# A two-layer RWKV-7/S5 trunk: solve columns moved to PSUM, lower weight parts reloaded, GpSimd's one-tensor operations given to ScalarE

## The chip, the cores and the metric

The kernel runs on one core of one Trainium2 chip. The metric is the device time of one execution in microseconds (us). TensorE is PE in the profile, VectorE is DVE, ScalarE is ACT, GpSimd is POOL and SyncE, which only issues DMAs here, is SP. Each of these engines works through its own instructions strictly in the order in which they were written; an instruction that has to wait for another engine holds up everything behind it on its own engine.

## The reference, cut to what matters

The input is 1024 tokens of 1024 channels in float32. Layer 0 is an RWKV-7 time mixer, layer 1 an S5 state-space mixer; each is followed by a squared-ReLU MLP of width 4096, and each sub-layer by a layer norm. The change lies in layer 0's mixer alone:

```python
xx = jnp.pad(x, ((0, 0), (1, 0), (0, 0)))[:, :-1] - x
xr = x + xx * mu[0]                      # likewise xw, xk, xv, xa, xg
r = xr @ wr
w_pre = (w0 + jnp.tanh(xw @ w1) @ w2).astype(f32)
decay = jnp.exp(-jnp.exp(-jax.nn.softplus(-w_pre) - 0.5))
k = xk @ wk
v = xv @ wv
a = jax.nn.sigmoid(a0 + (xa @ a1) @ a2)
g = jax.nn.sigmoid(xg @ g1) @ g2
k = k * (1.0 + (a - 1.0) * k_a)
def step(state, inp):
    r_t, w_t, k_t, v_t, a_t, b_t = inp
    sa = jnp.einsum('bhvk,bhk->bhv', state, a_t)
    state = (state * w_t[:, :, None, :] + sa[..., None] * b_t[:, :, None, :]
             + v_t[..., None] * k_t[:, :, None, :])
    return state, jnp.einsum('bhvk,bhk->bhv', state, r_t)
_, o = lax.scan(step, s0, seq_in)
```

The recurrence is not run token by token. It is cut into chunks of 64 tokens, and what the tokens of a chunk do to each other is a triangular system that is solved for each chunk and head.

## The kernel before, in words

**Products in two parts.** Every large matrix product takes its operands as an upper part (float32 rounded to the PE's fast format) and a lower part (what the rounding left). `wload` fetches a block of 128x512 weights into `wraw`, ScalarE copies it to the upper part `whi` (L146), VectorE subtracts to get the lower part `wlo` (L147), and `mm3` issues three matmuls (L175): upper by upper, upper by lower, lower by upper. Two buffers hold `wraw`, three `whi` and three `wlo`. All weights are fetched in this way each time they are used, 720 blocks in all.

**Two halves.** The tokens are treated as two halves of 512. `rwkv_proj(0)` and `rwkv_proj(1)` make the projections of each half with the same weights: `rates` (the decay and `a`, two weight blocks a half), `gate` (two), `square` (`wk` and `wr`, 16 blocks each) and the products with `wv` (16): 52 blocks a half that the change concerns. `mixes` makes the shifted inputs, x times (1 - mu) on ScalarE (L266) plus the shifted x times mu, either in one operation on VectorE (L268) or in two on GpSimd (L271, L272). `half_sigmoid` (L325) turns a tanh into a sigmoid on GpSimd. Results go to DRAM (`scr`) and come back for the recurrence.

**Eight units.** The recurrence runs in eight units, each of 256 tokens and 8 of the 16 heads. For each unit `elem` loads r, k, sg and a from `scr` (L485) and scales them, among others with `a` times k_a plus `kam` on GpSimd (L527); `amat` makes the triangular matrices; `invert` solves them; `chain` carries the state over the chunks (PE pR L672, pX L677, pU L682, with ScalarE and VectorE copies between them, L668 to L679); `gnorm` normalises the result, mostly on GpSimd (L733 to L739).

**The solve.** `invert` handles diagonal blocks of 32 by 32. The solved columns `xh` lie in half of the SBUF tile `x1`. Thirty steps of two VectorE operations follow: a product of a matrix column `xa` and solved rows into `tmp` (L608) and its addition to the rows below (L610), of 15 to 128 elements a partition. After that come two transposes (L614, L615), small matmuls into a PSUM tile `pv1` of pool `pl` (one buffer, tag "l"), and copies. The layer norms use the same buffer for `pm`, `pq` and `pr`.

**What sets the order.** A scheduler orders each engine's instructions by priorities (`rank`) and a model of their times; dependencies between rotating buffers follow the order in which the program names them. The projections of the second half, the output product `wo(0)` and the MLP have low priority, so they fill PE between the steps of the units. The units end at about 1060 us of the span; the MLPs, the S5 mixer and its products follow.

Of the kernel before, what the change touches and what calls it, by code (L numbers as in the profile page):

```python
# [8 lines left out]
F32 = mybir.dt.float32  # L9
# [9 lines left out]
HT = 512  # L19
# [51 lines left out]
def trunk(ctx, tc, A):  # L71
# [32 lines left out]
    V.tensor_scalar(kam, pv[:, PV.index("k_a")], -1.0, 1.0, op0=ALU.mult, op1=ALU.add)  # L104

    mum = cp.tile([128, 6, KT], F32, name="mum")
    V.tensor_scalar(mum, pv[:, 0:6], -1.0, 1.0, op0=ALU.mult, op1=ALU.add)

    def vec(n, k):
        i = PV.index(n)  # L110
        return pv[:, i, k : k + 1]
# [45 lines left out]

    def wload(src, kt, n):
        step = 512 // n
        out = []  # L160
        for k0 in range(0, kt, step):
            raw = wp.tile([128, step, n], F32, tag="wraw", name="wraw", bufs=2)
            SP.dma_start(raw, src[:, k0 : k0 + step])
            hi = wp.tile([128, step, n], F32R, tag="whi", name="whi")
            lo = wp.tile([128, step, n], F32R, tag="wlo", name="wlo")
            nw[0] += 1
            split(raw, hi, lo, G if nw[0] % WLG[0] in WLG[1] and WLG[2] <= nw[0] < WLG[3] else V)
            out += [(hi[:, k], lo[:, k]) for k in range(step)]
        return out
# [59 lines left out]
    def rwkv_proj(H):  # L229
# [33 lines left out]
        def mixes(j, dst=None):  # L263
            for k in range(KT):
                m = tp.tile([128, HT], F32, tag="m", name="m")
                S.mul(m, xs[k][:, 1:], mum[:, j, k : k + 1])  # L266
                if k % 4 in VM[H]:
                    V.scalar_tensor_tensor(m, xs[k][:, 0:HT], vec(f"mu{j}", k), m, op0=ALU.mult, op1=ALU.add)  # L268
                else:
                    m2 = tp.tile([128, HT], F32, tag="ev", name="m2", bufs=3)  # L270
                    G.tensor_scalar(m2, xs[k][:, 0:HT], vec(f"mu{j}", k), None, op0=ALU.mult)  # L271
                    G.tensor_add(m, m, m2)  # L272
                if dst:
                    split(m, *dst[k])
                    yield dst[k]
                else:
                    yield operand(m)
# [46 lines left out]
        def half_sigmoid(t):  # L324
            G.tensor_scalar(t, t, 0.5, 0.5, op0=ALU.mult, op1=ALU.add)  # L325

# [42 lines left out]
        def rates(n):  # L369

            if n % 4 == 0:
                w2[0] = wload(A["wa2"][:, n // 4], 4, 128)
            pp = [psd(), psd()]
# [10 lines left out]
        def gate(n):  # L384
            if n % 4 == 0:
                wg[0] = wload(A["g2a"][:, n // 4], 4, 128)
                rawb = wp.tile([128, 512], F32, tag="wraw", name="w2raw", bufs=2)
# [12 lines left out]
        def square(wn, out, xm, n):  # L400
            p = psd()
            dense(p, wload(A[wn][n], KT, 128), xm)
            e = tp.tile([128, HT], F32, tag="ev", name="ev", bufs=3)
            S.copy(e, p)  # L404
            store_out(out, n, e)
# [34 lines left out]
        for cb in range(4):  # L440
            pp = [psd(), psd()]
            for k0 in range(0, KT, 2):
                w = wload(A["wv"][cb][:, k0 : k0 + 2], 2, 256)
                for kk in range(2):
# [29 lines left out]
    def elem(m):  # L474
# [5 lines left out]
        for j in range(2):  # L480
# [45 lines left out]
            for i in range(2):  # L526
                G.tensor_scalar(kf[:, per(i)], a[:, per(i)], vec("k_a", n0 + i), kam[:, n0 + i : n0 + i + 1],  # L527
                                op0=ALU.mult, op1=ALU.add)
            G.tensor_mul(kf, kf, k)
# [55 lines left out]
    def invert(D):  # L585
# [5 lines left out]
        tmp = x1[:, 0].rearrange("p u j -> p (u j)")  # L591
        blk, xh = x1[:, 1], x1[:, 1].rearrange("p u j -> p (u j)")
        xv = xh.rearrange("p (t j) -> p t j", t=32)
# [771 lines left out]
```

## Time and profile before

| what | value |
|---|---|
| median of 3 runs | 2771.85 us (2769.56 to 2778.86) |
| the profiled execution's own time | 2764.91 us |
| its span, first to last instruction | 2763.2 us |
| its mean granted PE clock | 0.958 |
| PE matmul busy | 2604.9 us, 94% of the span |
| VectorE busy | 1884.5 us, 68% |
| ScalarE busy | 1109.5 us, 40% |
| GpSimd busy | 719.6 us, 26% |

A busy share is an average over stages, and PE counts as busy while a matmul is in its pipeline, at whatever clock. So the table says that PE is the engine to look at, and not yet where it loses time. The views used below are busy times by stretches of the span (us, then each engine's busy us and instruction count, then the granted PE clock, the DMA share and GB/s), groups of instructions (`x` count, busy us, mean ns, then the engine's idle time before them), one line's durations as min/median/max in ns, and the waits (us in total, times, longest).

### The profile page before, as it was taken

Reading aid. Unit: us, or ns where it says so; the run is one execution under the profiler, and the core shown is the slowest. Engines: PE = TensorE matmul, PEld = TensorE weight load, DVE = VectorE, ACT = ScalarE, POOL = GpSimd, SP = SyncE. Lnnn points to the kernel's source line nnn. Section 1 sums busy time; section 2 is a strip of 40 time slices with the busy share of each in tenths; the row PEclk is TensorE's granted clock in tenths of the full one; section 3 lists DMA queues with packets and bytes.
Section 4 is the critical chain, followed back from the end, with each engine's and each line's share of the span. In section 5 each row is a group of like instructions: output and inputs, shape, how many; then the busy total and the mean of one; then the engine's idle time right before and its main releaser. Section 6 shows DMA issues by size and latency. Waiting matters only on the chain.

```text
span 2763.2 us, 43707 instructions
## 1 busy us (share of the span) xinstructions
PE 2604.9 (94%) x16582; PEld 2096.5 (76%) x16582; DVE 1884.5 (68%) x3242; ACT 1109.5 (40%) x1952; POOL 719.6 (26%) x601
## 2 busy tenths in 40 slices
PE   7889989889899999989999999999999999999997
PEld 5779767678677877767776788778778887788886
DVE  7487788587787777998658554574765546755556
ACT  5445454544443333334432332344323323533333
POOL 5331664450352303233122001121220101210101
PEclk9989969889889999999999999999999999999998
DMA  3543443344222323555332633223343322333333
GB/s 115 184 147 112 139 162 102 109 138 135 77 81 81 100 85 124 154 145 159 96 122 99 203 96 98 89 88 102 117 160 112 99 96 84 119 96 97 98 95 100
DMA packets 200083, 318.63 MB, mean 115 GB/s; under 512 B 19520, under 2 KB 73920, under 8 KB 199872
## 3 DMA queue, kind: packets, MB, share of 16 engines
q1 hardware_dynamic: 199872, 315.83, 36.6%
q8 instruction: 131, 2.15, 0.3%
q14 instruction: 80, 0.66, 0.1%
HBM read 265.42 MB, written 50.33 MB: 114 GB/s over the span
## 4 chain that ended last, share of the span: by engine, by line
PE 45%; DVE 5%; issue 2%; POOL 1%; DMA 1%; ACT 0%; ACTq 0%; DVEq 0%; POOLq 0%
PE d L175 40%; PE py L1219 1%; PE py L1224 1%; DVE wlo L147 1%; PE pu L152 1%; DVE t L1187 1%; PE pbu L1175 1%; DVE hA L960 0%; DVE hB L960 0%; DVE t L1185 0%; POOL rl L944 0%; PE pq L849 0%; DMA wraw<-in_mw_dram 0%; PE pu L1164 0%; DVE qbuf L147 0%
## 5 line engine op out<-in xcount | busy, mean ns | idle before, releaser
L147 DVE TENSOR_TENSOR wlo<-wraw,whi 128x512 fp32r<-128x512 f32 x720 | 535.6, 745 | 443.7 <-ACT whi L146 424.8
L146 ACT CAST whi<-wraw 128x512 fp32r<-128x512 f32 x720 | 445.7, 620 | 975.4 <-PE d L175 637.2
L175 PE MATMUL d<-qbuf,whi 128*128 128x512 f32 (+1 forms) x2112 | 655.6, 393 | 20.9 <-DVE hA L960 9.4
L175 PEld LDWEIGHTS d<-qbuf,whi 128*128 128x128 f32 x2112 | 390.3, 190 | 117.7 <-DVE hA L960 17.0
L944 POOL TENSOR_TENSOR rl<-rl 128x512 f32<-128x512 f32 x128 | 158.6, 1239 | 1058.4 <-ACT rl L943 1018.1
L175 PE MATMUL d<-qbuf,wlo 128*128 128x512 f32 (+1 forms) x1056 | 409.3, 390 | 8.2 <-DVE wlo L147 8.0
L175 PE MATMUL d<-oAh,whi 128*128 128x512 f32 (+1 forms) x960 | 387.8, 408 | 9.6 <-ACT ev L404 7.2
L175 PE MATMUL d<-oAh,wlo 128*128 128x512 f32 (+1 forms) x960 | 387.2, 406 | 5.3 <-DVE wlo L147 5.1
L175 PE MATMUL d<-oAl,whi 128*128 128x512 f32 (+1 forms) x960 | 385.5, 404 | 1.4 <-DVE oAl L147 1.4
L175 PE MATMUL d<-oBh,wlo 128*128 128x512 f32 x704 | 278.3, 396 | 1.4 <-DVE wlo L147 1.4
L175 PE MATMUL d<-oBh,whi 128*128 128x512 f32 x704 | 278.8, 396 | 0.0
L175 PE MATMUL d<-oBl,whi 128*128 128x512 f32 x704 | 276.1, 392 | 0.0
L175 PEld LDWEIGHTS d<-qbuf,wlo 128*128 128x128 f32 x1056 | 200.6, 190 | 52.8 <-DVE wlo L147 11.7
L175 PEld LDWEIGHTS d<-oAh,whi 128*128 128x128 f32 (+1 forms) x960 | 185.1, 194 | 54.2 <-ACT ev L404 9.2
L175 PEld LDWEIGHTS d<-oAh,wlo 128*128 128x128 f32 (+1 forms) x960 | 184.9, 193 | 49.1 <-DVE wlo L147 8.6
L175 PEld LDWEIGHTS d<-oAl,whi 128*128 128x128 f32 (+1 forms) x960 | 184.8, 193 | 40.6 <-DVE oAl L147 2.1
L960 DVE TENSOR_TENSOR hB<-hB,d 128x512 f32<-128x512 f32 (+1 forms) x256 | 165.2, 650 | 68.9 <-PE d L175 65.8
L960 DVE TENSOR_TENSOR hA<-hA,d 128x512 f32<-128x512 f32 x240 | 162.5, 683 | 54.5 <-PE d L175 52.5
L175 PEld LDWEIGHTS d<-oBh,wlo 128*128 128x128 f32 x704 | 132.5, 188 | 33.8 <-DVE wlo L147 2.0
L175 PEld LDWEIGHTS d<-oBl,whi 128*128 128x128 f32 x704 | 132.7, 188 | 29.4 <-issue 0.5
L175 PEld LDWEIGHTS d<-oBh,whi 128*128 128x128 f32 x704 | 132.7, 189 | 29.1 <-issue 1.5
L147 DVE TENSOR_TENSOR qbuf<-rl,qbuf 128x512 fp32r<-128x512 f32 x128 | 99.0, 774 | 70.3 <-ACT qbuf L146 69.8
(371 smaller groups left out, 3877.1 us busy)
## 6 DMA issues: line engine op xcount, KB each, us to landing
wraw<-in_mw_dram SPq DMA_DIRECT2D x520, 256.0 KB, 2.7
wraw<-in_glu_dram SPq DMA_DIRECT2D x64, 256.0 KB, 2.6
wraw<-in_wk_dram SPq DMA_DIRECT2D x32, 256.0 KB, 3.1
wraw<-in_wr_dram SPq DMA_DIRECT2D x32, 256.0 KB, 3.1
wraw<-in_wv_dram SPq DMA_DIRECT2D x32, 256.0 KB, 3.4
yl<-s_y SPq DMA_DIRECT2D x32, 256.0 KB, 3.1
wraw<-in_wo_dram SPq DMA_DIRECT2D x32, 256.0 KB, 2.8
tb<-tB SPq DMA_DIRECT2D x16, 512.0 KB, 4.9
```

The source lines that it names most:

```text
L146: S.copy(hi, src)
L147: (e or V).tensor_sub(lo, src, hi.bitcast(F32))
L152: PE.matmul(out, x, idt, start=True, stop=True)
L175: bulk.append((PE.matmul(p, w, x, **kw).ins, x.shape[-1]))
L944: G.tensor_mul(r, r, r)
L960: V.tensor_add(z, z, p)
L1175: PE.matmul(p[qs, g2, ri], tb[:, g2, ri, qs], u[:, 2 * g2 + par], start=True, stop=True)
L1187: e.tensor_mul(t2[:, :, ri], x[:, :, 1 - ri], bw[:, l, g0:g1, ri : ri + 1].broadcast_to([128, g1 - g0, n]))
L1219: PE.matmul(p[64 * j : 64 * j + 64, g2], ug[f][:, 2 * g2 + par], tv[:, par, g2], start=g2 == 0, stop=False, skip_group_check=True)
L1224: PE.matmul(p[64 * j : 64 * j + 64, g2], hb[qs, 4 * f + g2, ri, 0:NSC], tcm[qs, g2, ri], start=False, stop=ri == 1, skip_group_check=True)
```

## The change

Four edits, all in layer 0's mixer:

1. `invert` takes `xh` from the PSUM pool `pl` (tag "l", the one buffer it shares with `pv1` and the layer norms' tiles). Before, `xh` was half of `x1`.
2. `wload` gets a key. The first time a block with a key is loaded (first half), its lower part is stored to a DRAM tile `low`. The second time (second half) the lower part is loaded from there into `wlo`, and VectorE's subtraction is left out; ScalarE still makes the upper part.
3. Of `mixes`, the multiplication by mu moves from GpSimd to ScalarE (18 instructions); the addition stays on GpSimd.
4. `half_sigmoid` (36 instructions) and the scaling of `a` in `elem` (32) move from GpSimd to ScalarE, the first with a constant tile `half` as its bias.

```diff
+    half = cp.tile([128, 1], F32, name="half")
+    V.memset(half, 0.5)
...
-    def wload(src, kt, n):
+    low = {}
+
+    def wload(src, kt, n, key=None):
...
+            kept = low.get((key, k0)) if key else None
             raw = wp.tile([128, step, n], F32, tag="wraw", name="wraw", bufs=2)
             SP.dma_start(raw, src[:, k0 : k0 + step])
...
-            split(raw, hi, lo, G if nw[0] % WLG[0] in WLG[1] and WLG[2] <= nw[0] < WLG[3] else V)
+            if kept is not None:
+                SP.dma_start(lo.bitcast(F32).rearrange("p k n -> p (k n)"), kept)
+                S.copy(hi, raw)
+            else:
+                split(raw, hi, lo, G if nw[0] % WLG[0] in WLG[1] and WLG[2] <= nw[0] < WLG[3] else V)
+                if key:
+                    low[key, k0] = dr.tile([128, 512], F32, name=f"low{len(low)}")
+                    SP.dma_start(low[key, k0], lo.bitcast(F32).rearrange("p k n -> p (k n)"))
...
-                    G.tensor_scalar(m2, xs[k][:, 0:HT], vec(f"mu{j}", k), None, op0=ALU.mult)
+                    S.mul(m2, xs[k][:, 0:HT], vec(f"mu{j}", k))
...
-            G.tensor_scalar(t, t, 0.5, 0.5, op0=ALU.mult, op1=ALU.add)
+            S.activation(t, t, AF.Identity, bias=half, scale=0.5)
...
-            dense(p, wload(A[wn][n], KT, 128), xm)
+            dense(p, wload(A[wn][n], KT, 128, f"{wn}{n}"), xm)
...
-                G.tensor_scalar(kf[:, per(i)], a[:, per(i)], vec("k_a", n0 + i), kam[:, n0 + i : n0 + i + 1],
-                                op0=ALU.mult, op1=ALU.add)
+                S.activation(kf[:, per(i)], a[:, per(i)], AF.Identity, bias=kam[:, n0 + i : n0 + i + 1],
+                             scale=vec("k_a", n0 + i))
...
-        blk, xh = x1[:, 1], x1[:, 1].rearrange("p u j -> p (u j)")
+        blk = x1[:, 1]
+
+        xh = pl.tile([128, HT], F32, tag="l", name="xh")
```

The loads for `rates`, `gate` and `wv` get keys in the same way as that of `square`.

The scheduler orders anew. On VectorE, in the solve of the fourth unit (`x_` is the tile `x1`, `wlo` a weight block's lower part), the program had before:

```order
L608 TENSOR_TENSOR x_4040<-xa,x_4040 128x110
L610 TENSOR_TENSOR x_4040<-x_4040 128x22x5
L147 TENSOR_TENSOR wlo<-wraw,whi 128x512
L608 TENSOR_TENSOR x_4040<-xa,x_4040 128x105
L610 TENSOR_TENSOR x_4040<-x_4040 128x21x5
L685 TENSOR_TENSOR st<-pU,st 128x256
L147 TENSOR_TENSOR wlo<-wraw,whi 128x512
L608 TENSOR_TENSOR x_4040<-xa,x_4040 128x120
L686 TENSOR_TENSOR st<-st,PL 128x256
L610 TENSOR_TENSOR x_4040<-x_4040 128x20x6
```

At the same steps of the same solve it now has:

```order
L623 TENSOR_TENSOR x_4149<-xa,xh 128x110
L625 TENSOR_TENSOR xh<-xh,x_4149 128x22x5
L623 TENSOR_TENSOR x_4149<-xa,xh 128x105
L625 TENSOR_TENSOR xh<-xh,x_4149 128x21x5
L623 TENSOR_TENSOR x_4149<-xa,xh 128x120
L700 TENSOR_TENSOR st<-pU,st 128x256
L625 TENSOR_TENSOR xh<-xh,x_4149 128x20x6
L701 TENSOR_TENSOR st<-st,PL 128x256
```

The subtractions for the second half's weights no longer stand between the steps, and each step has one SBUF input and one PSUM input where it had two from SBUF. From the first to the last step of this solve 30 other instructions stood between before, 8 do now.

On SP, in the second half's products with `wk` (`s_k` is k's place in DRAM, `vsa`, `ldk`, `lg`, `gt` loads for the units), the program had before:

```order
L163 DMA wraw<-in_wk_dram 128x512 x3
L365 DMA s_k<-ev 128x512
L163 DMA wraw<-in_wk_dram 128x512
L365 DMA s_k<-ev 128x512
L163 DMA wraw<-in_wk_dram 128x512
L365 DMA s_k<-ev 128x512
L485 DMA ldk<-s_k 128x2x256
L163 DMA wraw<-in_wk_dram 128x512
L749 DMA s_y<-gt 128x4x128
```

It now has:

```order
L498 DMA ldk<-s_k 128x2x256
L174 DMA wlo<-low_750 128x512
L169 DMA wraw<-in_wk_dram 128x512
L174 DMA wlo<-low_1319 128x512
L169 DMA wraw<-in_wk_dram 128x512
L669 DMA vsa<-s_v 64x2x256 x2
L378 DMA s_k<-ev 128x512
L174 DMA wlo<-low_1327 128x512
L169 DMA wraw<-in_wk_dram 128x512
```

Each weight block brings two loads instead of one, and the loads and stores of the units stand in the same queue behind them. Over the whole program SP issues 104 DMAs more, ScalarE has 86 instructions more, GpSimd 86 fewer and VectorE 51 fewer (52 subtractions gone, one constant added).

More of the change, by code (lines that the diff above doesn't have):

```diff
@@ L371, in rates @@
             if n % 4 == 0:
-                w2[0] = wload(A["wa2"][:, n // 4], 4, 128)
+                w2[0] = wload(A["wa2"][:, n // 4], 4, 128, f"wa2{n}")
             pp = [psd(), psd()]
@@ L385, in gate @@
             if n % 4 == 0:
-                wg[0] = wload(A["g2a"][:, n // 4], 4, 128)
+                wg[0] = wload(A["g2a"][:, n // 4], 4, 128, f"g2a{n}")
                 rawb = wp.tile([128, 512], F32, tag="wraw", name="w2raw", bufs=2)
@@ L442, in rwkv_proj @@
             for k0 in range(0, KT, 2):
-                w = wload(A["wv"][cb][:, k0 : k0 + 2], 2, 256)
+                w = wload(A["wv"][cb][:, k0 : k0 + 2], 2, 256, f"wv{cb}-{k0}")
                 for kk in range(2):
```

## The prediction

> **What bounds the kernel now.** I read busy times by stretches first, because the change touches only the part that ends at about 1060 us.
>
> ```profile
> 30.00:150.00 120.00, 108.05 (x529) 81.08 (x529) 62.95 (x92) 58.20 (x104) 42.97 (x45) 0.94 0.48 157
> 150.00:310.00 160.00, 147.91 (x1442) 128.58 (x1440) 124.09 (x260) 80.47 (x149) 56.56 (x49) 0.95 0.43 133
> 310.00:454.00 144.00, 125.18 (x1198) 97.62 (x1194) 122.76 (x221) 70.89 (x136) 85.28 (x77) 0.77 0.35 115
> 454.00:600.00 146.00, 127.17 (x1087) 103.94 (x1088) 102.25 (x187) 68.70 (x130) 69.41 (x52) 0.89 0.42 132
> 600.00:680.00 80.00, 76.46 (x735) 70.09 (x735) 61.17 (x137) 36.66 (x66) 14.28 (x14) 0.93 0.47 146
> 680.00:850.00 170.00, 151.04 (x1320) 121.58 (x1319) 147.24 (x264) 72.10 (x135) 80.70 (x64) 0.87 0.26 80
> 850.00:1060.00 210.00, 207.71 (x1638) 164.56 (x1638) 156.41 (x287) 80.32 (x148) 44.59 (x38) 1.00 0.30 93
> 1700.00:1750.00 50.00, 50.00 (x222) 41.44 (x221) 19.49 (x29) 13.84 (x24) 4.76 (x7) 1.00 0.30 98
> ```
>
> From 850 us on PE never stops for long and its clock is whole, so nothing saved there shortens the run. Between 30 and 850 us PE is idle for 820 - 735.8 = 84 us. Its clock is lower there too: busy time multiplied by what is missing of the clock gives 6.5 + 7.4 + 28.8 + 14.0 + 5.4 + 19.6 = 82 us. The stage thus loses about 166 us, half by waiting and half by the lower clock that goes with it. VectorE is busy 620 of these 820 us (76%), ScalarE 387 (47%). Next come PE's waits between 30 and 850 us, and one of ScalarE's.
>
> ```profile
> PE pU L682 <- ACT vsa L679: 14.5, 8, 4.6
> PE d L175 <- DVE oAl L147: 8.3, 5, 3.8
> PE d L175 <- ACT oAh L146: 8.3, 4, 5.3
> PE d L175 <- ACT ev L404: 7.2, 5, 4.0
> PE py L747 <- DVE st L685: 5.8, 2, 4.0
> PE pX L677 <- ACT o L674: 4.8, 3, 2.2
> PE d L175 <- DVE wlo L147: 4.2, 5, 1.3
> PE pss L507 <- DVE AT L570: 3.0, 1, 3.0
> ACT vsa L679 <- DVE vsa L678: 40.7, 18, 9.3
> ```
>
> The 14.5 us behind ScalarE's copy L679 are VectorE's, since that copy itself waited for VectorE's L678 (last row). I also count oAh, which waits for the mixed input that VectorE or GpSimd makes. Then 14.5 + 8.3 + 8.3 + 5.8 + 4.2 + 3.0 = 44.1 of the 84 us hang on VectorE's queue, 52%; with the same share of the clock's 82 us that is **87 us**. One such wait in order of time shows the mechanism (start, duration):
>
> ```profile
> 372.21 2.15 POOL L733 TENSOR_TENSOR vt<-vsa,bo 64x512 f32<-64x512 f32 x2
> 372.30 1.09 DVE L608 TENSOR_TENSOR x<-xa,x 128x117 f32<-128x117 f32 x1
> 373.43 1.08 DVE L610 TENSOR_TENSOR x<-x 128x117 f32<-128x117 f32 x1
> 374.54 0.28 DVE L608 TENSOR_TENSOR x<-xa,x 128x120 f32<-128x120 f32 x1
> ...
> 376.06 1.08 PE L747 MATMUL py<-ident,o 128*128 128x128 f32 x4 [4.04 <-DVE st L685]
> ```
>
> While GpSimd runs, two solve steps take 1.08 us each; as soon as it is done, one of the same size takes 0.28. PE waits 4.04 us for an addition (L685) that stands behind them.
>
> **The subtractions.** The window 310 to 690 us holds the second half's loads.
>
> ```profile
> L147 DVE TENSOR_TENSOR wlo<-wraw,whi 128x512 fp32r<-128x512 f32 x59 | 46.2, 786 | 30.4 <-ACT whi L146 30.2
> L147 DVE TENSOR_TENSOR wlo<-wraw,whi x720: 637/687/2799, 43.5 to 2737.8; 128x512 fp32r<-128x512 f32 x180
> L860 DVE TENSOR_TENSOR hA<-hA,pr x32: 679/681/687, 771.3 to 2409.4; 128x512 f32<-128x512 f32 x32
> ```
>
> 52 of them go, at 786 ns each: **41 us** of VectorE. The last two rows show why PSUM matters: with two SBUF inputs this size takes up to 2799 ns, with one input in PSUM never more than 687.
>
> **The solve.** These are its two lines, one size of theirs in all eight units, and a pair of equal size with and without a PSUM input.
>
> ```profile
> L610 DVE TENSOR_TENSOR x<-x 128x30 f32<-128x30 f32 (+7 forms) x240 | 83.2, 347 | 5.1
> L608 DVE TENSOR_TENSOR x<-xa,x 128x30 f32<-128x30 f32 (+7 forms) x240 | 70.2, 292 | 5.0
> L608 DVE TENSOR_TENSOR x<-xa,x 128x84 f32<-128x84 f32 x8 | 1.9, 242 | 0.1
> L686 DVE TENSOR_TENSOR st<-st,PL 128x256 f32<-128x256 f32 x28 | 13.9, 498 | 0.6
> L685 DVE TENSOR_TENSOR st<-pU,st 128x256 f32<-128x256 f32 x28 | 11.8, 421 | 4.4 <-PE pU L682 4.0
> L678 DVE COPY vsa<-pX 64x256 f32<-64x256 f32 x32 | 13.7, 428 | 12.1 <-PE pX L677 11.3
> L669 DVE COPY vsa<-st x32: 291/291/1360, 178.1 to 1054.2; 64x256 f32<-64x256 f32 x32
> ```
>
> The thirty sizes average 86 elements, and 84 take 242 ns undisturbed. 480 steps would then take 116 us; they take 153. With one PSUM input each, 37 us of disturbance should go. The eighth unit, after 850 us, is one of eight but met little of GpSimd, so I take **34 us**. The unknown is the price of PSUM in a short operation, above all of writing it, which no row shows. Below, it could be nothing or a small gain (421 against 498 in the pair above). Above, I take the copies: 428 from PSUM, 291 from SBUF, 137 ns more, times 480 is 66 us. I take nothing, since the addition is nearer to these steps than a copy; both ends stay for the range.
>
> The Trainium skill speaks against this edit: Perfetto Trace Analysis, section Optimizing Scalar/DVE Operations, puts VectorE's fixed access at about 60 ns in SBUF and 125 in PSUM. By that rule an estimate is 65 ns times 480, 31 us more, and nearly all of the edit's gain is gone. The trace doesn't show it for a PSUM input (421 against 498 ns); for a PSUM output no row here can tell.
>
> Nothing is late in its place: the shared PSUM buffer's other users lie elsewhere. The one layer norm among the units ends its reads before the seventh solve begins, and `pv1` follows the transpose that reads `xh` last in any case.
>
> **GpSimd's operations.** The rows are those of the moved instructions, and of ScalarE's nearest ones.
>
> ```profile
> L271 POOL TENSOR_SCALAR m<-xs,pv 128x512 f32<-128x512 f32 x18 | 32.1, 1792 | 14.3 <-DMA s_k<-ev 4.4 <-PE d L343 3.0 <-DVE oS L147 2.7
> L325 POOL TENSOR_SCALAR ev<-ev 128x512 f32<-128x512 f32 x32 | 22.7, 720 | 32.4 <-ACT ev L380 24.6 <-issue 7.8
> L527 POOL TENSOR_SCALAR kf<-lda,pv,kam 128x256 f32<-128x256 f32 x32 | 24.7, 777 | 45.7 <-DMA lda<-s_a 23.7 <-PE pX L677 7.1 <-PE pT L580 6.4
> L266 ACT ACTIVATE m<-xs,mum 128x512 f32<-128x512 f32 x48 | 33.8, 719 | 17.1 <-DVE oAl L147 16.2 <-DVE stash L147 0.6
> L503 ACT ACTIVATE kk<-ldk,pv 128x256 f32<-128x256 f32 x32 | 14.5, 501 | 32.3 <-POOL lda L534 15.3 <-DVE AR L533 8.5 <-DMA ldk<-s_k 8.4
> ```
>
> GpSimd loses 80 us (four more of L325 beside). ScalarE gains 54 x 0.72 + 32 x 0.50 = 55 us. That GpSimd runs less relieves VectorE's other SBUF operations by something between 0 and these 80 us; I take **10**, because one-input operations need less of SBUF than the two-input ones that ran in the wait above. The latency of a mixed input falls by 1792 - 719 = 1.07 us, 18 times, 19 us; I take 8 us of PE's waits, about what oAh has, and 8 of clock with it.
>
> **The sum.** VectorE loses 41 + 34 + 10 = 85 of 620 us and its load in the stage falls from 76% to 65%. How far PE's 87 us shrink no row tells; the bounds are 0 (VectorE only idles more) and all 85 us one for one. I take a queue's rule of thumb, waits in proportion to load over idle share, 3.1 before and 1.9 after: 40% less, **35 us**. Add 16 for the mixes. Against it stands ScalarE, from 47 to 54%: by the same rule the waits shown that are its own (ev and o, 12 us) grow by a third, 4 us and 4 of clock. The net is 35 + 16 - 8 = **43 us**. The profiled execution took 2764.9 us, 1.7 beyond its span, so it becomes 2722; the median of the runs shown, 2771.85, lies 7 us higher, and I forecast it at **2729 us**.
>
> The DMAs are costed at nothing.
>
> ```profile
> wraw<-in_wk_dram SPq DMA_DIRECT2D x32, 256.0 KB, 3.1
> q1 hardware_dynamic: 199872, 315.83, 36.6%
> ```
>
> 52 stores and 52 loads of 256 KB are 27 MB on 316, which at the same rate is 3.2% of the engines' span, 88 us, spread over 650 us whose DMA share is 0.35 to 0.48. A store waits for the subtraction that also frees `wraw` for the next load, a wait that SP had already. A load of a lower part must wait until PE has left the `wlo` three blocks back. A block is 12 matmuls, at 222 in 50 us 2.7 us, so two blocks in hand give 5.4 us; from issue to landing such a load takes 3.1. The cover is 2.3 us a block; without it each further us costs 48 us, a block of k, r and v each.
>
> **Rivals.**
> - *The freed time doesn't reach PE.* The units' chain runs through PE, ScalarE and VectorE (pR, o, pX, vsa, pU), and VectorE's gaps only grow. For it: VectorE is idle for 24% of the stage already, and 48% of PE's idle time does not name it. What stays is the mixes' 16 less ScalarE's 8 and a little of the solve: 5 to 15 us, about 2762.
> - *PSUM has its price.* With 66 us of it VectorE loses only 19 us; the same rule gives a load of 73%, 11% less of 87, 10 us, and 18 us in sum: 2754. Against it speaks L685.
> - *SP's queue becomes the bound*, which ends slower. What stands ahead of a lower part in SP's queue waits itself, a store of k for its `ev` for instance. If that exceeds the cover by more than 0.9 us a block, 48 x 0.9 = 43 us, the gain is gone. At 1.3 us beyond it 62 us are lost, 19 more than gained: 2791. The units' loads behind it (`vsa`, `ldk`) come late too. For it: in the order after, such stores and loads do stand between the lower parts. Against it: a lower part stands right beside a `wraw`, whose wait is nearly the same.
> - *More than forecast.* If VectorE sets the pace, 85 us go one for one, with the mixes' 16 less ScalarE's 8: 93 us, 2679.
>
> **How the numbers follow.** Forecast 0.57 (2700 to 2750), freed time not on PE 0.15, SP's queue 0.13, more 0.08, PSUM's price 0.07. Within 0.3%, about what a measurement can tell from no change, is 2763.5 to 2780.2. Faster: 0.57 + 0.08, with about 0.08 of the first rival and 0.04 of PSUM's, is 0.77; the same 0.10; slower 0.13. The range 2688 to 2775 leaves out half of the largest gain and SP's case.
>
> **What would show it.** In the profile after, L623 and L625 should average near 245 ns, none above 0.6 us; at 380 PSUM has its price. VectorE's busy time between 30 and 850 us should fall by some 85 us, PE's idle time by a quarter, and the granted clock between 310 and 600 should rise. If PE waits for `wlo<-low` DMAs, SP's queue is the bound. If VectorE's busy time falls and PE's idle time does not, the first rival holds. The stage after 1060 us should be unchanged within 5 us; if it isn't, the new order there outweighs what I have costed.

## The result, and the profile after

The changed kernel takes 2753.36 us (median of 10 runs, 2745.29 to 2757.5), the kernel before 2770.7 beside it (10 runs): a ratio of 0.9941, 95% interval 0.9928 to 0.9954. The change gains 0.6%, some 16 us. The forecast had the sign and its range holds the time, but it was 43 us, so the size is off by more than half. The profiled execution took 2756.91 us, with a span of 2755.1.

The busy times by stretches of the changed kernel, the stages of the prediction first and the whole of 30 to 850 us last (columns: stretch, then busy us and count of PE, PE's weight loads, VectorE, ScalarE, GpSimd; granted clock, DMA share, GB/s):

```profile
30.00:150.00 120.00, 108.67 (x531) 82.52 (x530) 59.99 (x89) 69.29 (x122) 21.49 (x19) 0.91 0.60 199
150.00:310.00 160.00, 150.77 (x1376) 131.82 (x1375) 117.63 (x256) 87.36 (x162) 42.74 (x42) 0.91 0.58 182
310.00:454.00 144.00, 120.89 (x1177) 95.16 (x1175) 99.16 (x195) 91.12 (x172) 60.30 (x46) 0.82 0.47 151
454.00:600.00 146.00, 130.78 (x1172) 104.84 (x1171) 88.36 (x173) 72.51 (x136) 53.62 (x43) 0.89 0.56 172
600.00:680.00 80.00, 77.56 (x799) 70.54 (x799) 58.47 (x152) 40.44 (x75) 11.38 (x11) 0.97 0.62 191
680.00:850.00 170.00, 155.32 (x1409) 126.58 (x1410) 141.12 (x267) 79.60 (x148) 76.35 (x60) 0.85 0.26 80
30.00:850.00 820.00, 743.99 (x6455) 611.46 (x6455) 564.72 (x1128) 440.31 (x812) 265.88 (x217) 0.89 0.50 157
```

VectorE is relieved: 565 us where it was busy for 620, and over the whole run 1811.4 us where it was 1884.5, 73 us less. PE hardly notices: its idle time is 820 - 744.0 = 76 us (before 84), and busy time times what is missing of the clock is 9.8 + 13.6 + 21.8 + 14.4 + 2.3 + 23.3 = 85 us (before 82; with a clock of two digits such a sum is no finer than 4 us). The first two stretches have far more transfers, a DMA share of 0.58 to 0.60 where it was 0.43 to 0.48. Their clock of 0.91, where it was 0.94 and 0.95, is this execution's own: in a second profile of the same kernel (e17 below) they have 0.94 and 0.96 at a share of 0.60.

The waits of PE between 30 and 850 us (us in total, times, longest), with the one of ScalarE that the prediction followed:

```profile
PE d L188 <- ACT ev L417: 8.4, 5, 3.0
PE d L188 <- DVE oAl L149: 7.6, 5, 3.6
PE d L188 <- ACT oAh L148: 7.1, 5, 3.3
PE pA L580 <- DVE AT L583: 6.4, 3, 3.3
PE pn L528 <- ACT sq L525: 5.1, 3, 3.0
PE d L188 <- ACT ev L393: 4.2, 2, 2.9
PE pv L644 <- ACT x L640: 3.6, 1, 3.6
PE d L188 <- DMA wlo<-low: 2.7, 2, 2.4
PE d L188 <- DVE wlo L149: 2.4, 2, 1.3
PE pU L697 <- ACT vsa L694: 0.4, 2, 0.2
ACT vsa L694 <- DVE vsa L693: 21.7, 11, 6.5
```

The six waits that the prediction linked to VectorE were 44.1 us. Four of them are left here with 7.6 + 7.1 + 2.4 + 0.4 = 17.5; the other two are gone. So 27 us of just these waits went, yet PE's idle time fell by only 8. Others came in their place, at the small products of the units (`pA`, `pn`, `pv`) and behind ScalarE's `ev`, 8.4 + 4.2 us in two lines that had 7.2 and 0.2 before.

The solve (one line's min/median/max in ns, then both lines as groups, then one size in all eight units), and the subtractions:

```profile
L623 DVE TENSOR_TENSOR x<-xa,xh x240: 161/252/290, 160.4 to 970.4; 128x30 f32<-128x30 f32 x16, 128x56 f32<-128x56 f32 x16, 128x78 f32<-128x78 f32 x16, 128x96 f32<-128x96 f32 x16
L625 DVE TENSOR_TENSOR xh<-xh,x x240: 168/264/300, 160.6 to 970.6; 128x30 f32<-128x30 f32 x16, 128x56 f32<-128x56 f32 x16, 128x78 f32<-128x78 f32 x16, 128x96 f32<-128x96 f32 x16
L623 DVE TENSOR_TENSOR x<-xa,xh 128x30 f32<-128x30 f32 (+7 forms) x240 | 58.5, 244 | 5.6
L625 DVE TENSOR_TENSOR xh<-xh,x 128x30 f32<-128x30 f32 (+7 forms) x240 | 60.7, 253 | 5.3
L623 DVE TENSOR_TENSOR x<-xa,xh 128x84 f32<-128x84 f32 x8 | 1.9, 238 | 0.2
L625 DVE TENSOR_TENSOR xh<-xh,x 128x84 f32<-128x84 f32 x8 | 2.0, 249 | 0.1
L149 DVE TENSOR_TENSOR wlo<-wraw,whi 128x512 fp32r<-128x512 f32 x668 | 497.8, 746 | 432.6 <-ACT whi L148 412.7
```

The solve takes 58.5 + 60.7 = 119 us instead of 153, and no step is longer than 300 ns. By the start and end times in the two traces, 109 of the 480 steps before ran beside a GpSimd instruction, and 44 of these took over 0.4 us, up to 2.24; of the other 371 none took more than 0.3. Now 120 run beside one and take 244 ns in the mean. The moved multiplication of the mixes, and what GpSimd still does behind it:

```profile
L284 ACT ACTIVATE m<-xs,pv 128x512 f32<-128x512 f32 x18 | 12.4, 719 | 1.0 <-DMA s_g<-ev 0.5 <-DMA s_k<-ev 0.4
L285 POOL TENSOR_TENSOR m<-m,m 128x512 f32<-128x512 f32 x18 | 26.6, 1479 | 58.7 <-ACT m L279 28.3 <-ACT m L284 24.7 <-DMA lg<-in_lnx_dram 5.7
```

Last the DMA issues (KB each, us from issue to landing):

```profile
low<-wlo SPq DMA_DIRECT2D x52, 256.0 KB, 2.7
wlo<-low SPq DMA_DIRECT2D x52, 256.0 KB, 3.5
wraw<-in_wk_dram SPq DMA_DIRECT2D x32, 256.0 KB, 3.6
wraw<-in_wv_dram SPq DMA_DIRECT2D x32, 256.0 KB, 4.2
```

`wk` blocks landed after 3.1 us before and 3.6 now, `wv` blocks after 3.4 and 4.2. The prediction had looked for waits on the new DMAs and costed them at nothing otherwise; that the other loads get slower beside them is the first hint of what follows.

### The profile page after: what moved, and what is told of

Its sections match the earlier page's. It is cut to its first block, busy times and chain, and to the rows that moved or that the text cites. A ratio compares the mean times of both kernels' runs of the same rounds, so it can differ in the third digit from the quotient of the medians.

```text
span 2755.1 us, 43773 instructions
## 1 busy us (share of the span) xinstructions
PE 2602.8 (94%) x16582; PEld 2099.3 (76%) x16582; DVE 1811.4 (66%) x3191; ACT 1156.3 (42%) x2038; POOL 628.2 (23%) x515
## 3 DMA queue, kind: packets, MB, share of 16 engines
q1 hardware_dynamic: 214848, 343.10, 40.2%
## 4 chain that ended last, share of the span: by engine, by line
PE 63%; DVE 12%; DMA 5%; issue 4%; ACT 2%; POOL 1%; SPq 0%; ACTq 0%; DVEq 0%; POOLq 0%
PE d L188 53%; DVE wlo L149 2%; DMA wraw<-in_mw_dram 2%; PE py L1234 1%; PE pA L580 1%; PE py L1239 1%; DMA yl<-s_y 1%; DVE hA L975 1%; PE pbu L1190 1%; PE pu L154 1%; PE pR L687 1%; PE pX L692 0%; POOL rl L959 0%; ACT whi L148 0%; DVE t L1202 0%
## 5 line engine op out<-in xcount | busy, mean ns | idle before, releaser
L148 ACT CAST whi<-wraw 128x512 fp32r<-128x512 f32 x668 | 413.6, 620 | 932.0 <-PE d L188 625.0
L149 DVE TENSOR_TENSOR wlo<-wraw,whi 128x512 fp32r<-128x512 f32 x668 | 497.8, 746 | 432.6 <-ACT whi L148 412.7
L188 PE MATMUL d<-qbuf,whi 128*128 128x512 f32 (+1 forms) x2112 | 655.0, 393 | 20.5 <-DVE hA L975 7.7
L188 PEld LDWEIGHTS d<-qbuf,whi 128*128 128x128 f32 x2112 | 390.7, 190 | 115.2 <-DVE hA L975 14.6
L188 PE MATMUL d<-qbuf,wlo 128*128 128x512 f32 (+1 forms) x1056 | 409.5, 390 | 9.5 <-DVE wlo L149 9.3
L188 PE MATMUL d<-oAh,whi 128*128 128x512 f32 (+1 forms) x960 | 394.4, 414 | 21.0 <-ACT ev L417 8.4
L188 PE MATMUL d<-oAl,whi 128*128 128x512 f32 (+1 forms) x960 | 390.6, 408 | 5.6 <-DVE oAl L149 5.6
L188 PE MATMUL d<-oAh,wlo 128*128 128x512 f32 (+1 forms) x960 | 390.2, 407 | 5.8 <-DVE wlo L149 3.4
L188 PE MATMUL d<-oBh,whi 128*128 128x512 f32 x704 | 278.6, 396 | 0.0
L188 PE MATMUL d<-oBh,wlo 128*128 128x512 f32 x704 | 277.7, 395 | 0.0
L188 PE MATMUL d<-oBl,whi 128*128 128x512 f32 x704 | 276.4, 393 | 0.0
L188 PEld LDWEIGHTS d<-qbuf,wlo 128*128 128x128 f32 x1056 | 200.0, 190 | 55.1 <-DVE wlo L149 13.6
L188 PEld LDWEIGHTS d<-oAh,whi 128*128 128x128 f32 (+1 forms) x960 | 188.0, 196 | 66.5 <-ACT ev L417 10.2
L188 PEld LDWEIGHTS d<-oAh,wlo 128*128 128x128 f32 (+1 forms) x960 | 188.2, 196 | 49.9 <-DVE wlo L149 5.1
L188 PEld LDWEIGHTS d<-oAl,whi 128*128 128x128 f32 (+1 forms) x960 | 188.4, 196 | 46.9 <-DVE oAl L149 7.8
L188 PEld LDWEIGHTS d<-oBh,wlo 128*128 128x128 f32 x704 | 132.5, 188 | 32.1 <-issue 2.0
L188 PEld LDWEIGHTS d<-oBl,whi 128*128 128x128 f32 x704 | 132.6, 188 | 29.9 <-issue 0.9
L188 PEld LDWEIGHTS d<-oBh,whi 128*128 128x128 f32 x704 | 132.8, 189 | 28.2 <-issue 0.7
```

Of the source, the lines that this page charges most:

```text
L148: S.copy(hi, src)
L149: (e or V).tensor_sub(lo, src, hi.bitcast(F32))
L188: bulk.append((PE.matmul(p, w, x, **kw).ins, x.shape[-1]))
```

## The experiments

A ratio is always to the kernel before, run on the same chip in between, with its 95% interval; 0.001 is 2.8 us. Two kinds have to be kept apart. In *its own order* the scheduler orders the kernel anew after the edit, so the edit and a new order come together. In a *held order* the instructions that both kernels have are tied, on each engine, to the order of before or of the changed kernel by dependencies that only order them; just what the edit adds is free to move. The instructions in which the two kernels differ, the 52 subtractions and the 86 one-tensor operations among them, are placed by the scheduler in these runs. Where an edit leaves them as they were, that moves little: against the trace of before, e9 has two of GpSimd's instructions and one of VectorE's elsewhere, e10 14 and e11 24 of VectorE's.

### Single edits, each in its own order

The solve alone (`invert` as in the change, nothing else):

```diff
-        blk, xh = x1[:, 1], x1[:, 1].rearrange("p u j -> p (u j)")
+        blk = x1[:, 1]
+        xh = pl.tile([128, HT], F32, tag="l", name="xh")
```

> Only the solve's columns in PSUM, the rest as before. VectorE should lose 34 us, all of it in the units' stage. Theory A (VectorE's relief reaches PE, and the reloaded weight parts give it back): 12 to 20 us faster than before. Theory B (the relief mostly widens VectorE's own gaps): 2 to 8 us faster.

Measured: 0.9979 (0.9965 to 0.9994), 6 us faster.

The reloaded lower parts alone (the `wload` part of the change and its keys, nothing else):

> Only the reloaded lower parts, the rest as before. VectorE should lose 38 us. Theory A: the 104 DMAs, in SP's queue and on the DMA engines, give back all that: between 5 us faster and 10 us slower than before. Theory B: 2 to 8 us faster, as the loads cost nothing.

Measured: 1.0039 (1.0022 to 1.0056), 11 us slower, although VectorE does 52 subtractions less.

The solve together with the 86 operations on ScalarE, without the reload:

> The solve in PSUM and GpSimd's one-tensor operations on ScalarE, without the reloaded parts. Theory A: faster than the whole change, by 10 to 20 us (25 to 37 us faster than before). Theory B: slower than the whole change, by 2 to 8 us (9 to 15 us faster than before).

Measured: 0.9947 (0.9921 to 0.9973), 15 us faster.

And the subtractions left out at no price at all:

```diff
             if kept is not None:
-                SP.dma_start(lo.bitcast(F32).rearrange("p k n -> p (k n)"), kept)
                 S.copy(hi, raw)
+                lo = hi
```

with no stores either; the second half's products take the upper part in place of the lower one.

> The rest as before, but the second half's 52 blocks take their upper part a second time in place of the lower: no subtraction, no store, no load, the same matmuls. This is the reload at no price. Theory A: 15 to 25 us faster than before, and so 15 us or more better than the reload alone. Theory B: the same as the reload alone within 4 us, 2 to 8 us faster than before.

Measured: 1.0024 (1.0007 to 1.0041). By this run the freed time of VectorE would be worth nothing, the first rival. The held orders below show that this reading is wrong: what the subtractions gave, the scheduler's new order took (the traces of e4 and e9 below show where).

### The changed kernel's order, with one edit taken back at a time

All edits undone, the order of the changed kernel held:

> All edits undone, but every instruction that both kernels have stands in the order of the changed kernel, on every engine; the subtractions and GpSimd's operations are placed by the scheduler. If the new order carries the gain: 8 us or more faster than before. If the edits carry it: between 5 us faster and 15 us slower than before, since this order expects faster engines than it gets.

Measured: 1.0002 (0.9986 to 1.0018). The new order by itself carries no time, but it isn't without effect. The last product of the units on PE is a transpose into `py` (start, duration), here before and in the changed kernel:

```profile
1090.91 0.60 PE L747 MATMUL py<-ident,o 128*128 128x128 f32 x4
```

```profile
1064.08 0.60 PE L762 MATMUL py<-ident,o 128*128 128x128 f32 x4
```

So the units end at 1065 us in the changed kernel, 27 us earlier than before (1091 us; the 1060 named at the start is too early), and yet its span is only 8 us shorter, because what follows the units takes 1690 us instead of 1672: 60 of PE's instructions that stood ahead of the units' end now stand behind it. With the order alone, in e5, the units end at 1075 us and the rest takes 1692. The order thus shortens the units by 16 us and lengthens what follows by 20. Under this order, what edits gain is how much earlier than 1075 us the units end: 1057 to 1065 in the two profiles of the changed kernel and in e6, e7 and e8, with 1687 to 1694 us behind them (one profile each; the changed kernel's two differ by 6 us). e4, in its own order, has lost its gain in the same way: its units end at 1082 us as in e9 below, but 1689 us follow, where e9 has 1674.

Solve back in SBUF, the rest as in the changed kernel:

> The changed kernel in exactly its own order, with the solved columns back in SBUF. Forecast's theory: VectorE gains 34 us of work and the run gets 12 to 20 us slower than the changed kernel. Rival (VectorE's time is mostly off PE's path): 2 to 8 us slower.

Lower parts subtracted again, no stores and no loads:

> The changed kernel in its own order, but with the second half's 52 lower parts subtracted on VectorE again, no stores and no loads. Forecast's theory: 12 to 20 us slower than the changed kernel. Rival (the DMAs cost more than the subtractions saved): 5 to 15 us faster, the first half's end (about 271 us in the changed kernel) earlier by 5 us or more.

The 86 operations back on GpSimd:

> The changed kernel in its own order, but with the 86 one-tensor operations back on GpSimd. Forecast's theory: 8 to 12 us slower than the changed kernel. Rival (they are worth more, since GpSimd's queue and its share of SBUF hold VectorE): 15 to 25 us slower.

| taken back | ratio | interval | against the changed kernel's 0.9941 |
|---|---|---|---|
| solve (e6) | 0.9974 | 0.9957 to 0.9990 | +0.0033, 9 us slower without it |
| reload (e7) | 0.9930 | 0.9909 to 0.9950 | -0.0011, 3 us faster without it |
| GpSimd's operations (e8) | 0.9934 | 0.9914 to 0.9955 | -0.0007, 2 us faster without it |

Each difference has an error of some 6 us, so only the solve's stands out. Of the change's 16 us the solve carries about 9 here; neither the reload nor the operations on ScalarE are seen to earn anything when they alone are taken back. That leaves some 7 us which no single edit accounts for.

### What a subtraction is worth, in the order of before

The same edit as in e4, every common instruction held in the order of before:

> Kernel before, every engine's common instructions kept in the order of before; only the 52 subtractions of the second half are left out (its products take the upper part in place of the lower one: same matmuls, no store, no load). VectorE is relieved of 52 x 0.79 = 41 us between 30 and 850 us with no price anywhere. Prediction's sum (queue rule on the 41 of 85 us): about -17 us (ratio 0.994). VectorE sets the pace: -30 to -41 us (0.985 to 0.989). Rival (freed VectorE time doesn't reach PE): within +-5 us (0.998 to 1.002), VectorE's busy time 35 us lower and PE's idle time between 30 and 850 us unchanged.

Each of the 52 subtractions done twice:

```diff
                 S.copy(hi, raw)
                 V.tensor_sub(lo, raw, hi.bitcast(F32))
+                V.tensor_sub(lo, raw, hi.bitcast(F32))
```

> Kernel before in its own order, with each of the second half's 52 subtractions done twice: VectorE gets 41 us or more of work. Queue rule (load 76 to 81 per cent, waits in proportion to load over idle share, 3.1 to 4.3): 87 x 0.36 = +31 us (1.011). VectorE sets the pace: +41 us or more (1.015). Rival (VectorE's time there lies off PE's path): within +-6 us (0.998 to 1.002).

And PE relieved instead of VectorE: one of three matmuls (upper weights by lower input) left out in the second half's products with `wk`, `wr` and `wv`:

```diff
     def mm3(p, whi, wlo, xh, xl, first, last):
         mmb(p, whi, xh, start=first, stop=False)
-        mmb(p, whi, xl, start=False, stop=False)
+        if not second[0]:
+            mmb(p, whi, xl, start=False, stop=False)
         mmb(p, wlo, xh, start=False, stop=last)
```

> Kernel before in its own order; in the second half's products with wk, wr and wv one of the three matmuls (upper weights by lower input) is left out, 256 instructions, about 45 us of PE work at its steady pace (0.23 us for 512 columns, half that for 256). If the second half's products only fill PE's gaps and the units' chain sets the end of the stage: within +-8 us. If the amount of PE work sets the end and what VectorE saves only moves gaps: -35 to -45 us (0.984 to 0.987). In between: some of the removed work turns into idle time.

Measured: without the subtractions 0.9957 (0.9943 to 0.9970), 12 us faster; with them doubled 1.0109 (1.0090 to 1.0127), 30 us slower; with 256 matmuls less 0.9984 (0.9969 to 1.0000), 4 us faster. The stage from 30 to 850 us, as one row of the busy times. Before:

```profile
30.00:850.00 820.00, 735.82 (x6297) 602.90 (x6297) 620.45 (x1157) 387.02 (x716) 349.20 (x299) 0.89 0.39 123
```

Without the subtractions (e9), and with them doubled (e10):

```profile
30.00:850.00 820.00, 732.10 (x6325) 599.63 (x6324) 594.92 (x1128) 388.97 (x720) 346.29 (x300) 0.90 0.39 124
```

```profile
30.00:850.00 820.00, 718.21 (x6112) 589.34 (x6110) 624.37 (x1157) 377.47 (x698) 334.70 (x284) 0.87 0.38 120
```

With fewer matmuls (e11):

```profile
30.00:850.00 820.00, 703.58 (x6009) 571.25 (x6007) 613.25 (x1145) 384.90 (x713) 342.89 (x294) 0.86 0.39 123
```

The last row is the striking one. PE does 32 us less in this stage than before, and idles for 116 us instead of 84, at a clock of 0.86 instead of 0.89. Some of that is this execution's own: it took 2777.55 us, 15 more than the kernel's median, and its first half, in which no matmul was left out, ends 15 us later than that of before (the last product with `wv` at 283.3 us instead of 268.5). But the ratio of all runs gives only 4 us, where an estimated 45 us of matmuls were taken out. So PE's work doesn't set the end of the stage. What does is the end of the units: in the profiles of e9 to e16 the units end between 1082 and 1124 us, and the rest takes 1667 to 1677 us in each. So the prediction's "166 us lost" were no stock to draw on. Nor does the gain of e9 show as idle time saved: PE idles for 88 us here, and before for 84.

Why doubling costs more than leaving out gives is seen in PE's wait for a lower part (4.2 us before). Doubled (e10, L188 is the second subtraction; with the wait behind `vsa`, 14.5 us before), and left out (e9, where L151 makes the lower parts that are still subtracted):

```profile
PE d L200 <- DVE wlo L188: 22.2, 7, 8.4
PE pU L710 <- ACT vsa L707: 11.8, 6, 4.6
```

```profile
PE d L198 <- DVE wlo L151: 1.4, 3, 0.9
```

Before, PE hardly waits for a lower part, so there was little to win; with two subtractions a block it waits 22 us. That is the only one of the six waits linked to VectorE that grew; the other five have 33 us where they had 40. So e10 doesn't show that a fuller VectorE makes everything behind it late. It shows that PE, which works in order, is held up by lower parts that come later. Neither do e9 and e10 separate two things that one subtraction does: it takes VectorE's time, and it is a step on a block's way from `wraw` to PE. The solve taken back (e6) changes only the first, and that is worth 9 us with 6 of error.

### What the stores and loads cost, in the order of before

Reload alone, order of before held:

> Kernel before with its common instructions in the order of before, and only the second half's lower parts reloaded (52 stores, 52 loads, no subtractions). Against e9 it adds just the DMAs and the waits on SP. If these cost nothing, as the prediction took them: the time of e9 within 4 us. If the stores hold up SP's queue in the first half: 5 to 12 us above e9, with the end of the first half's wv products later by about as much. If the loads wait for wlo (SP's queue as the bound): PE waits on the reloaded lower parts above 15 us.

Only the 52 stores (second half as in e9):

> e9 (before's order, no subtractions in the second half, which takes the upper part as lower) with only the 52 stores of the first half added, nothing loaded. Theory that the stores delay the first half's weight loads: most of the 19 us that e12 lies above e9, ratio to before 1.000 to 1.003, and the first half's last wv product 5 us or more later than in e9. Rival (the loads carry it, by waiting for wlo in SP's queue): as e9, 0.994 to 0.997.

Only the 52 loads, all from one tile that a single store filled, so that the second half's lower parts are those of one block:

> e9 with only the 52 loads of the second half added; all read one tile that a single store has filled, so the bytes and the waits on wlo are those of e12 and the values are not. Theory that the stores carry the price: within 4 us of e9, 0.994 to 0.998. Rival (loads): 1.000 to 1.003, with PE waiting for the loaded lower parts or SP waiting for PE by 10 us or more beyond e9.

Stores and loads of a quarter of the bytes; the second half's products read that quarter of the lower part four times over:

```diff
-                    low[key, k0] = dr.tile([128, 512], F32, name=f"low{len(low)}")
-                    SP.dma_start(low[key, k0], lo.bitcast(F32).rearrange("p k n -> p (k n)"))
+                    low[key, k0] = dr.tile([128, 128], F32, name=f"low{len(low)}")
+                    SP.dma_start(low[key, k0], lo.bitcast(F32).rearrange("p k n -> p (k n)")[:, 0:128])
```

> e12 with each of the 52 stores and loads cut to 128 of 512 columns (64 KB instead of 256; the second half's products read this quarter four times over, same matmuls): same DMAs, same places and waits in SP's queue, a quarter of the bytes. If bytes beside the weights' loads make the price (DMA share 0.61 against 0.46 in 30 to 150 us): three quarters of the 19 us go, ratio 0.996 to 0.999. If the waits in SP's queue make it: as e12, 1.001 to 1.004.

e9 and e12 were measured on one chip, e13 to e15 on another, each beside the kernel before.

| kernel, order of before | ratio | interval | above e9 |
|---|---|---|---|
| no subtractions (e9) | 0.9957 | 0.9943 to 0.9970 | |
| + stores and loads of a quarter (e15) | 0.9983 | 0.9967 to 1.0000 | 7 us |
| + stores (e13) | 0.9991 | 0.9975 to 1.0007 | 9 us |
| + loads (e14) | 0.9999 | 0.9981 to 1.0017 | 12 us |
| + stores and loads (e12) | 1.0025 | 1.0011 to 1.0039 | 19 us |

With 0.002, 5 to 6 us, of error on each difference, the two halves of the price add up: 9 + 12 is about the 19. My expectation that the stores carry most of it missed; the loads cost at least as much. And three quarters of the bytes make 12 of the 19 us (1.0025 - 0.9983), so most of the price is in the bytes and not in the waits of SP's queue, which e15 has all the same. SP's wait until PE has left a `wlo`, which e9 doesn't have, in e12 and in e15:

```profile
SPq L186 <- PE d L201: 71.7, 21, 11.3
```

```profile
SPq L186 <- PE d L207: 73.8, 24, 11.7
```

What e15 keeps, 7 us, is more than the quarter of the bytes would give, but not by more than its error; what these waits of SP cost, if anything, lies within it.

Where the bytes are felt is the wait of ScalarE, which makes the upper parts, for a weight block. The second half's copies are L185 in e9 and L187 in e12, the first half's L150 in both. The waits of e9 between 30 and 850 us for blocks of `wk`, `wr` and `wv`:

```profile
ACT whi L185 <- DMA wraw<-in_wk_dram: 11.0, 5, 3.9
ACT whi L185 <- DMA wraw<-in_wv_dram: 10.2, 4, 4.2
ACT whi L185 <- DMA wraw<-in_wr_dram: 7.5, 3, 3.8
ACT whi L150 <- DMA wraw<-in_wv_dram: 6.9, 2, 3.7
ACT whi L150 <- DMA wraw<-in_wr_dram: 1.8, 1, 1.8
ACT whi L150 <- DMA wraw<-in_wk_dram: 0.5, 1, 0.5
```

And those of e12:

```profile
ACT whi L187 <- DMA wraw<-in_wk_dram: 13.7, 5, 4.5
ACT whi L187 <- DMA wraw<-in_wv_dram: 13.4, 5, 4.5
ACT whi L187 <- DMA wraw<-in_wr_dram: 10.2, 5, 3.9
ACT whi L150 <- DMA wraw<-in_wv_dram: 10.0, 3, 5.9
ACT whi L150 <- DMA wraw<-in_wk_dram: 7.1, 4, 3.6
ACT whi L150 <- DMA wraw<-in_wr_dram: 4.9, 2, 3.2
```

That is 37.9 us in e9 and 59.3 in e12. The same six rows add up to 44.9 in e15, 51.3 in e13 and 52.0 in e14: the same order as the times, and 0, 7, 13, 14 and 21 us above e9 where the prices are 0, 7, 9, 12 and 19. The match to the microsecond is luck, since the sums are of one profile each and leave out the blocks of other weights that ScalarE waits for in the same stretch. With those of `wo` and `mw` (L150) the sums are 50.4 (e9), 49.4 (e15), 57.6 (e13), 58.2 (e14) and 68.5 (e12), and e15 no longer lies above e9. Nor is the wait the price itself: the kernel before has 32.7 us of it for the three weights and is slower than e9. That the bytes cost time is shown by e15; that they cost it through this wait is likely, not shown. The blocks do land later, as the weights' loads show (min/median/max from issue to landing; the first line is for 30 to 290 us, the second for 290 to 690). In e9:

```profile
DMA to landing us min/median/max: 2.5/3.0/4.6
DMA to landing us min/median/max: 2.5/3.6/6.2
```

In e12, with stores and loads:

```profile
DMA to landing us min/median/max: 2.8/3.6/5.2
DMA to landing us min/median/max: 2.5/4.0/6.2
```

In e15, with a quarter of their bytes:

```profile
DMA to landing us min/median/max: 2.6/3.2/4.5
DMA to landing us min/median/max: 2.5/3.6/6.6
```

In the first half, where the stores go, the median rises from 3.0 to 3.6 us; in the second, where the loads go, from 3.6 to 4.0. With a quarter of the bytes it is back at 3.2 and 3.6. The Trainium skill, DMA: Bandwidth & Descriptors, section Latency and other measured facts, gives the access latency of HBM as 0.2 us on average and 2 us at high load. No run here shows that latency by itself; what the traces show is the whole time from issue to landing, and it grows with the load, by 0.4 to 0.6 us in the median at a DMA share of 0.53 to 0.58 (e12) against 0.41 to 0.45 (e9).

### The operations on ScalarE, and the reload once more

The 86 operations on ScalarE, the order of before held:

> Kernel before in its own order with only the 86 GpSimd operations of mixes, half_sigmoid and elem on ScalarE. Prediction's terms (16 for the mixes, 4 of VectorE's 10 by the queue rule, less 8 for ScalarE): -12 us, ratio 0.9957. Rival (the engine of these operations hardly matters, ScalarE gets as late as GpSimd gets free): within 4 us, 0.9985 to 1.0015.

Measured: 0.9993 (0.9978 to 1.0007), 2 us. GpSimd's busy time falls from 720 to 639 us and VectorE's from 1884.5 to 1873.1, 11 us where 10 were forecast; neither is seen in the time.

The changed kernel and e7's version of it, side by side on one chip:

> The changed kernel once more, beside e18 on one chip. Result so far 0.9941. By the reload's net price at the order of before (+19 for DMAs, -12 for subtractions) it should be 7 us (0.0025) above e18; if the reload is free in the new order, equal to it within 3 us.

> e7 once more (changed kernel in its own order, second half's lower parts subtracted, no stores or loads). By the reload's net price 0.9916 if e17 is 0.9941; if the reload is free there, the same as e17.

Measured: 0.9945 (0.9927 to 0.9964) with the reload, 0.9930 (0.9910 to 0.9951) without, medians 2750.63 and 2747.41 us. Both pairs (0.9941 and 0.9930 the first time, then not side by side) have the kernel without the reload ahead by 3 to 4 us. By its ratio it is the fastest version found: surely faster than before, and ahead of the changed kernel by less than the error.

## Why the prediction was right in sign and wrong in size

**Subtractions: right.** 41 us of VectorE were forecast to go. The group `wlo<-wraw,whi` fell from 535.6 to 497.8 us, 38 us. The queue's rule made 35 x 41 / 85 = 17 us of time out of it; e9 measured 12, with 4 of error. For the doubled subtractions the rule said 31 us, and e10 measured 30. That the rule fits both is partly luck. It lets all waits grow or shrink with VectorE's load, by 36% in e10, but there one wait grew by 18 us and the other five shrank, and in e9 the six shrank by some 4 of 44 us only. The first rival (the freed time doesn't reach PE) is wrong for this edit, though e4 seemed to show it: leaving the subtractions out does make the run faster, be it by VectorE's free time or by the shorter way of a block.

**DMAs: the step that failed.** "The DMAs are costed at nothing" was wrong by 19 us (5 of error) in the order of before, more than the subtractions give. In the changed kernel subtractions and DMAs together should have been worth 17 us; taking them back (e7) made it 3 us faster. That is 20 of the 27 us that the forecast was too large, with some 6 of error. I had asked only whether a load of a lower part comes in time: it does, PE's wait for `wlo<-low` is 2.7 us. SP does wait for PE, by 72 us in e12, but the rival of SP's queue, in which the lower parts come late by it, did not happen. Not asked was what 27 MB do to the 256 KB weight loads beside them, in a stage whose DMA share stood at 0.35 to 0.48 already and where ScalarE waited for `wraw` before.

**Solve: size right on VectorE, perhaps less in time.** 34 us were forecast and 153.4 - 119.2 = 34 measured. By the rule this is 35 x 34 / 85 = 14 us of time; e1 shows 6 (own order, 4 of error) and e6 shows 9 (6 of error, so 14 is not excluded). PSUM has almost no price here: the line that writes it averages 253 ns against 244 for the line that writes SBUF, 2 us in 240 steps. The estimate of 31 us by the Trainium skill (Perfetto Trace Analysis, section Optimizing Scalar/DVE Operations) does not hold for these steps: 84 elements take 238 ns with a PSUM input and 249 with PSUM input and output, against 242 in SBUF alone. The gain that I read from the pair 421 against 498 isn't one: 498 is a mean that GpSimd had lengthened, and the medians of the two lines are 425 and 424. What its SBUF — State Buffer page says in the section SBUF: two separate sides, that a VectorE operation with two SBUF inputs is blocked while GpSimd holds the port that they share, is what the traces show: up to 1.08 us in the quoted wait before, at most 300 ns now that one input is in PSUM. Not each GpSimd instruction does it: 28 steps before ran beside one of 128x8 elements (L510, L721) and took 239 ns in the mean, none over 0.3 us.

**GpSimd's operations: wrong.** 16 us for the mixes and 4 through VectorE (35 x 10 / 85), less 8 for ScalarE, make 12; e16 measured 2, with 4 of error. The 8 us of PE's waits were those for `oAh`, and these fell only from 8.3 to 7.1 us; the clock's 8 hung on them. The mix's latency did not fall as I took it: the addition on GpSimd now waits 24.7 us for ScalarE's `m` (L285), and became slower itself, from 1378 to 1479 ns.

**Losses of PE as a measure: wrong.** I read the stage as 166 us that PE loses and asked how much of it returns. e11 shows that they are no stock: of an estimated 45 us of matmuls taken out, 4 came back as time. The six waits linked to VectorE did shrink from 44.1 to 17.5 us, but others of the same chain grew. VectorE itself lost 73 us instead of 85: 38 + 34, and hardly any of the 10 that e16 shows alone. That PE never stops for long from 850 us on was read from two stretches and is too strong: between 1200 and 1250 us it was busy for 42 of 50 us, at a clock of 0.86. And the stage behind the units, which was to stay within 5 us, grew by 19, the forecast's own sign of a new order that was not costed; the units' earlier end outweighed it.

**What stays open.** The terms measured in the order of before or alone, 12 + 6 to 9 + 2 - 19, give a gain of only 1 to 4 us, and the change gains 16. In the changed kernel's order the reload costs 3 to 4 us instead of 7, and solve and operations together gain 19 us where 8 to 11 is their sum. Each of these differences is about as large as its error, and the order alone (e5) gives nothing. That the edits help each other, or that the new order suits them, is possible and was not shown. The solve in PSUM was not tried in the order of before.

## What to carry to other kernels

Replacing work by transfers has two prices, and asking whether the transfer comes in time covers one: the other is that every transfer beside it lands later, and it is to be looked for at the waits on DMAs that the kernel had before. Find out what sets the pace by thinning and by doubling one engine's work with the order held; PE's idle time and clock told less here than 256 matmuls left out. But a doubled instruction also makes its own result late, so look at which waits grew before the engine is called the bound. And let a scheduler's new order not stand for the edit's effect: the same edit was 0.24% slower in its own order and 0.43% faster in the held one, and the end of the units, compared with what follows it, shows which of the two it was.

## What the hardware showed that was not expected

- 52 stores and 52 loads of 256 KB, by which the DMA packets' share of the engines' span rose from 37.1% (e9) to 40.2% (e12), made the other loads of that size land 0.4 to 0.6 us later in the median, and cost 19 us.
- Writing PSUM in a short VectorE operation costs some 9 to 11 ns (253 against 244 in the mean, 249 against 238 at 84 elements).
- The granted clock fell where matmuls were taken out: 0.86 between 30 and 850 us with 256 matmuls less and 116 us idle (e11), 0.89 with 84 us idle before; over the whole run the median of its 12 executions is 0.950, that of 23 of the kernel before 0.958. The sum of PE's idle time alone doesn't give it: with 102 us idle it was 0.87 in e10 and 0.90 in e2.
- Two SBUF inputs left a solve step open to GpSimd: of 109 steps beside a GpSimd instruction 44 took over 0.4 us, up to 2.24, where 0.25 is usual; with one input in PSUM none of 120 did.
